# Second MLP product of an encoder layer: operands split in the units' order, weight sums issued four units ahead, and the last product's row tiles taken 0, 2, 1, 3

## The chip, the core and the metric
The kernel runs on one core of a Trainium2 chip. The metric is the device time of one execution in microseconds (us), as the median of several runs. Below, PE is the matrix engine, DVE the vector engine, ACT the scalar engine, POOL the general engine, and SP the engine whose queue issues most transfers.

## The reference
One layer of an encoder runs on two sequences of 512 rows and 1024 columns. After attention, retention and an output projection comes the MLP, and this change lies in its second product and in the final norm:

```python
h = rms_norm(x, norm2_g[l]) * (1.0 + sc2) + sh2
x = x + g2 * (jnp.square(jax.nn.relu(h @ w_mlp1[l])) @ w_mlp2[l])
return rms_norm(x, final_g)
```

The hidden width is 4096. All inputs are float32.

## The kernel before, in words
Every float32 product is made of three matmuls in a reduced format: an operand is split into a high part (a cast, on ACT) and a low part (source minus high part, on DVE), and high x high, high x low and low x high are added up in PSUM.

Both MLP products use a seven-product scheme for a 2 x 2 block split (Strassen's, in Winograd's form). The first product runs over 16 pairs of hidden tiles (`FirstPair`, PE line L933) and writes the seven combinations of the activations to DRAM (`spill`). The second product is the list `steps`: two groups g, in each the seven products in the order P1, P2, P6, P7, P5, P4, P3, and in each product NU = 4 units h. That makes 56 units, numbered n from 0. `multiply(n, t)` issues six matmuls of unit n for row tile t; a unit is 24 matmuls over four row tiles (L1291). The results stand in four PSUM tiles of two banks each: `x` and `y`, each for th = 0 (row tiles 0 and 1) and th = 1 (row tiles 2 and 3). P1, P6, P5 and P3 write `x`, the others `y`.

What a unit needs comes in three steps, each run ahead of it in the loop over n:
- `load_u(n + 4)` (L1248) loads the unit's activation `ur` from `spill`, and `load_w(n + 8)` (L1241) loads weight blocks. Only P1, P2 and P6 load: P1 block b11, P2 block b21, P6 blocks b12 and b22. All go through SP's queue.
- `prep(n + 2)` makes the operands. For a unit of P6 it first makes three sums of weight blocks on DVE (L1268 to L1270), for P7 one (L1272); P5, P4 and P3 reuse them. Then `split_pairs` splits activation (`uc_n_h`, `uc_n_l`) and weight (`wc_n_h`, `wc_n_l`): ACT line L838, DVE line L839.
- The split operands, the weight blocks and two of four sum tiles share a pool of 32 equal buffers (`r4`); four of them go to a unit's split.

A scheduler sets the order of the instructions on each engine here; program order is a preference, not a rule, except where `in_order` or `pin` fixes it. An engine takes its instructions strictly in that order.

After a product's last unit `gather` takes the bank: a copy on ACT (L1303) the first time, else an addition on DVE (L1305). In the last group the sums are multiplied by a gate row and added to the residual `x2r` (`gated`, L1332 and L1333), squared and summed along the row (`squares`: ACT L1338, POOL L1341), and scaled with the inverse root (`finish`: POOL L1345, then DVE L1352 or, for one half, ACT L1350) and stored (L1353, SP's queue).

The last product (P3 of group 1) is written out by row tiles: for each t in 0, 1, 2, 3 all four units, then `finish` of the rows that are ready, `gated`, `squares` and `finish(0, t)`. The pairs (i, t) name half and tile of the output rows. The order of this part is fixed by `pin`.

Of the kernel before, what the change touches and what calls it, by code (L numbers as in the profile page):

```python
# [13 lines left out]
ALU = mybir.AluOpType  # L14

P = 128
# [14 lines left out]
def trunk_kernel(ctx, tc, x0, x1, c0, c1, w_ada, b_ada, norm1_g, w_in, attn_sink, decay_f, decay_b,  # L31
                 w_out, norm2_g, w_mlp1, w_mlp2, final_g, y0, y1):
    nc = tc.nc
    xin = (x0[0], x1[0])
    yout = (y0[0], y1[0])
# [19 lines left out]
    def r4(name, dtype=F32R):  # L55
        return work.tile([P, 2, 512], dtype, tag="r4", name=name, bufs=N_R4)
# [7 lines left out]
    def junk(name):  # L64
        return work.tile([P, 1024], BF16, tag="f2", name=name, bufs=8)

    def small(shape, name, tag="small", bufs=24):
        return work.tile(shape, F32, tag=tag, name=name, bufs=bufs)

    def f(ap):  # L70
        return ap.bitcast(F32)
# [70 lines left out]
    neghalf = const.tile([P, 4], F32, name="neghalf")  # L142
# [9 lines left out]
    for r0, src in ((0, c0[0]), (8, c1[0]), (16, norm1_g[0]), (24, norm2_g[0]), (32, b_ada)):  # L152
        n = src.shape[0] // P
# [672 lines left out]
    P1, P2, P6, P7, P5, P4, P3 = range(7)  # L826
# [10 lines left out]
    def split_to(hi, lo, src):  # L837
        nc.scalar.copy(hi, src)  # L838
        nc.vector.tensor_sub(lo, src, f(hi))  # L839
# [21 lines left out]
    class FirstPair:  # L861
# [15 lines left out]
        def prep(self, p):  # L877
            r1, r2 = self.raw
            c = lambda t: t.rearrange("p (s k n) -> p s k n", s=2, n=P)
            w = lambda t: t.rearrange("p (k n) -> p k n", n=256)  # L880
            F1, F2 = slice(0, P), slice(P, 256)
            if p in (P1, P2):
                t = c(self.pair(f"a{p}", True))
                split_to(t[:, 0], t[:, 1], (r1 if p == P1 else r2)[:, :, F1])
                self.left[p] = t[:, 0], t[:, 1]
            elif p == P6:
                self.s1 = f2(f"ws1_{self.n}").rearrange("p (k n) -> p k n", n=P)
                nc.vector.tensor_tensor(self.s1, r1[:, :, F2], r2[:, :, F2], ALU.add)
                nc.vector.tensor_sub(r1[:, :, F2], r1[:, :, F1], r1[:, :, F2])
                nc.vector.tensor_sub(r1[:, :, F1], self.s1, r1[:, :, F1])  # L890
                h, l = w(self.pair("s2h", False)), w(self.pair("s2l", False))
                split_to(h, l, r1)
                self.left[P6] = h[:, :, F1], l[:, :, F1]
                self.left[P7] = h[:, :, F2], l[:, :, F2]
            elif p == P5:
                t = c(self.pair("s1", True))
                split_to(t[:, 0], t[:, 1], self.s1)
                self.left[P5] = t[:, 0], t[:, 1]
            elif p == P4:
                nc.vector.tensor_sub(r2[:, :, F1], r2[:, :, F1], r1[:, :, F1])  # L900
                h, l = w(self.pair("s4h", False)), w(self.pair("s4l", False))
                split_to(h, l, r2)
                self.left[P3] = h[:, :, F1], l[:, :, F1]
                self.left[P4] = h[:, :, F2], l[:, :, F2]
# [321 lines left out]
    steps = [(g, p, h) for g in range(NG) for p in ORDER for h in range(NU)]  # L1226
    blocks = {P1: [(0, 0)], P2: [(1, 0)], P6: [(0, 1), (1, 1)]}
    raw_w, raw_u, left, right, t1 = {}, {}, {}, {}, {}
    acc, fin = {}, {}
# [4 lines left out]
    def load_w(n):  # L1234
        if n >= len(steps):
            return
        g, p, h = steps[n]
        n0 = g * GP + 2 * h
        for k, j in blocks.get(p, ()):
            t = raw_w[g, k, j, h] = r4(f"w2_{g}_{h}_{k}{j}", F32)  # L1240
            nc.sync.dma_start(t, w_mlp2.rearrange("(n k p) c -> p n k c", k=2, p=P)[:, n0:n0 + 2, k, j * 512:(j + 1) * 512])  # L1241

    def load_u(n):
        if n >= len(steps):
            return
        g, p, h = steps[n]
        t = raw_u[n] = (r4 if n < NU else lx)(f"ur_{n}", F32)
        in_order(nc.sync.dma_start(t, spill[g][p, :, 2 * h:2 * h + 2, :]))  # L1248

    def split_pairs(name, src):  # L1250
        hi, lo = r4(f"{name}h"), r4(f"{name}l")
        split_to(hi, lo, src)
        return hi, lo

    def t1_tile(g, h):
        if h < 2:
            pool, tag, bufs = ((work, "raw", 3), (late, "ws2", 3))[h]
            return pool.tile([P, 2, 512], F32, tag=tag, name=f"t1_{g}_{h}", bufs=bufs)
        return r4(f"t1_{g}_{h}", F32)

    def prep(n):
        if n >= len(steps):
            return
        g, p, h = steps[n]
        b11, b12, b21, b22 = [raw_w.get((g, k, j, h)) for k in range(2) for j in range(2)]
        if p == P6:
            t = t1[g, h] = t1_tile(g, h)
            nc.vector.tensor_sub(t, b12, b11)  # L1268
            nc.vector.tensor_sub(b12, b22, b12)
            nc.vector.tensor_sub(b11, b22, t)  # L1270
        if p == P7:
            nc.vector.tensor_sub(b21, b21, b11)  # L1272
        src = {P1: b11, P2: b21, P6: b11, P7: b12, P5: t1.get((g, h)), P4: b21, P3: b22}[p]
        left[n] = split_pairs(f"uc_{n}_", raw_u.pop(n))
        right[n] = split_pairs(f"wc_{n}_", src)


    bank = {}
# [28 lines left out]
    def cols_of(j):  # L1307
        return slice(j * 512, (j + 1) * 512)
# [26 lines left out]
    def squares(q, t):  # L1335
        i, j = q
        ss = small([P, 1], f"ssf_{i}_{t}_{j}")
        nc.scalar.activation(junk(f"jkf_{i}_{t}_{j}")[:, :512], fin["x", i, t // 2, j][:, t % 2, :], AF.Square, accum_out=ss)  # L1338
        before = fin.get(("ms", i, t), EPS)
        ms = fin["ms", i, t] = small([P, 1], f"msf_{i}_{t}_{j}")  # L1340
        nc.gpsimd.tensor_scalar(ms, ss, 1.0 / D, before, ALU.mult, ALU.add)  # L1341

    def finish(i, t, gained=()):
        r = small([P, 1], f"rf_{i}_{t}")
        nc.gpsimd.tensor_tensor(r, fin["ms", i, t], neghalf[:, 0:1], ALU.pow)  # L1345
        r0 = i * 256 + (t % 2) * P
        for j in range(2):
            x = fin["x", i, t // 2, j][:, t % 2, :]
            if j in gained:
                nc.scalar.activation(x, x, AF.Copy, scale=r)  # L1350
            else:
                nc.vector.scalar_tensor_tensor(x, x, r, fin["f", j], ALU.mult, ALU.mult)  # L1352
            nc.sync.dma_start(yout[t // 2][r0:r0 + P, cols_of(j)], x)  # L1353


    ahead = {P1: lambda: (load_w(0), load_u(0), load_w(1), load_u(1)),
# [21 lines left out]
    for n, (g, p, h) in enumerate(steps[:-NU]):  # L1378
        final = g == NG - 1
        load_u(n + 4)  # L1380
        load_w(n + 8)
        prep(n + 2)
        if n + NU + 1 == len(steps):
            prep(n + 3)
            prep(n + 4)
        if final and h == 0:
            if p == P1:
                final_loads()
            elif p == P7:
                final_rows(0)  # L1390
            elif p == P5:
                final_rows(1)
        for t in range(4):
            src = multiply(n, t)
            th = t // 2
            if h < NU - 1 or t % 2 == 0:
                continue
            q = where[p]
            if not final or p in (P1, P6, P7):
                gather(p, th, src)  # L1400
            elif p == P2:
                gather(p, th, src)
            elif p == P5:
                gather(p, th, src)
                gated(q, th, acc[q, th])
            else:
                gated(q, th, src)
        if final and p in (P7, P5, P4) and h == NU - 1:
            if p == P7:
                for th in range(NB):  # L1410
                    gated((0, 0), th, acc[(0, 0), th])
                for t in range(4):
                    squares((0, 0), t)
            elif p == P5:
                for q in ((1, 0), (0, 1)):
                    for th in range(NB):
                        gated(q, th, acc[q, th])
                for t in range(4):
                    squares((1, 1), t)
            else:  # L1420
                for t in range(4):
                    squares((1, 0), t)
    start = len(nc.cur_bb.bb.instructions)
    for t in range(4):
        for n in range(len(steps) - NU, len(steps)):
            src = multiply(n, t)
        if t == 0:
            finish(1, 0)
            finish(1, 1)
        elif t == 1:  # L1430
            finish(1, 2)
            finish(1, 3)
        elif t == 3:
            x = fin["x", 0, 1, 0][:, 1, :]
            nc.vector.tensor_tensor(x, x, fin["f", 0], ALU.mult)
        gated((0, 1), t // 2, src[:, t % 2:t % 2 + 1, :], slice(t % 2, t % 2 + 1))
        squares((0, 1), t)
        finish(0, t, (0,) if t == 3 else ())
    pin(start)
    lates.close()  # L1440
    front.close()
# [27 lines left out]
```

## Time and profile before

| | |
|---|---|
| median of 3 runs | 1148.64 us (1148.45 to 1151.57) |
| the profiled execution | 1147.91 us, span 1145.2 us |
| PE busy | 1111.3 us, 97% of the span |
| DVE, ACT, POOL busy | 889.1, 506.8, 46.8 us |
| mean granted clock of PE | 0.991 |
| second product, first and last matmul | 819.2 and 1136.8 us |

The time outside the span is 2.7 us. Times below are microseconds from the start of the span. In a row of the timeline stand start, duration, engine, line, operation, output<-inputs and, in brackets, the idle time before it with what ended it. Matmuls overlap, so the step from one start to the next is what a matmul costs, not its duration. In names, buffer and unit numbers are left out (`wc_l<-w,wc_h`: the low part of a weight).

### The profile page before, as it was taken

To read this page: it belongs to the slowest core of one execution; us is meant where nothing else is said; L and a number is where in the kernel's file an instruction comes from. 1 tells how busy PE (TensorE), PEld (TensorE's weight loads), DVE (VectorE), ACT (ScalarE), POOL (GpSimd) and SP (SyncE) were. 2 spreads that over 40 slices of the span, in tenths; PEclk is the share of its full clock that TensorE was granted. 3 is DMA by queue.
4 is the path that set the end of the run, shared out by engine and by line. 5 is a ranking of instruction groups with operands and counts; after the bars stand their busy time and mean duration, and the time that the engine had idled before them with its cause. 6 is when DMAs were issued, how large, how long until landed. Compare 5 with 4: busy or idle time off the path is not lost.

```text
span 1145.2 us, 14502 instructions
## 1 busy us (share of the span) xinstructions
PE 1111.3 (97%) x5205; PEld 909.7 (79%) x5205; DVE 889.1 (78%) x1484; ACT 506.8 (44%) x860; POOL 46.8 (4%) x82
## 2 busy tenths in 40 slices
PE   7899999999999999999999999999989999999996
PEld 5688887778888778887888888888868888888875
DVE  6768888989878797689998779776768645688675
ACT  7737765444662334346333333333344542444341
POOL 2200001000000000100000000000000000000011
PEclk8999999999999999999999999999989999999998
DMA  9946767675555589941654445442883455524603
GB/s 309 377 179 206 236 207 278 190 230 177 164 174 186 163 307 346 320 147 49 220 200 157 169 168 187 157 165 102 307 315 104 138 201 196 199 91 167 194 14 142
DMA packets 124623, 224.36 MB, mean 196 GB/s; under 512 B 8500, under 2 KB 59780, under 8 KB 124552
## 3 DMA queue, kind: packets, MB, share of 16 engines
q1 hardware_dynamic: 122792, 217.09, 56.2%
q0 software_dynamic: 1632, 6.32, 1.5%
q8 instruction: 40, 0.66, 0.2%
q14 instruction: 31, 0.25, 0.1%
q10 hardware_dynamic: 128, 0.04, 0.0%
HBM read 152.36 MB, written 71.06 MB: 195 GB/s over the span
## 4 chain that ended last, share of the span: by engine, by line
PE 81%; DVE 8%; DMA 6%; ACT 2%; issue 2%; POOL 1%; SPq 0%; ACTq 0%; POOLq 0%; DVEq 0%
PE x L1291 13%; PE px_None L933 12%; PE y L1291 12%; PE py_None L933 9%; PE po L130 2%; PE po L131 2%; PE po L129 2%; PE po L421 2%; PE ppt L414 2%; PE psc L388 1%; DMA raw_ada<-in_w_ada_dram 1%; PE pj_rv L129 1%; PE pj_rv L130 1%; PE pj_rv L131 1%; PE pj_rg L129 1%
## 5 line engine op out<-in xcount | busy, mean ns | idle before, releaser
L839 DVE TENSOR_TENSOR uc_l<-ur,uc_h 128x1024 fp32r<-128x1024 f32 x56 | 68.3, 1220 | 49.0 <-ACT uc_h L838 31.9
L1291 PE MATMUL x<-wc_h,uc_h 128*128 128x512 f32 x256 | 100.4, 393 | 3.7 <-DVE acc L1332 3.7
L1291 PE MATMUL x<-wc_l,uc_h 128*128 128x512 f32 x256 | 100.2, 391 | 0.0
L1291 PE MATMUL x<-wc_h,uc_l 128*128 128x512 f32 x256 | 100.1, 391 | 0.0
L838 ACT CAST uc_h<-ur 128x1024 fp32r<-128x1024 f32 x56 | 58.8, 1050 | 77.5 <-PE x L1291 22.7
L1291 PE MATMUL y<-wc_l,uc_h 128*128 128x512 f32 x192 | 76.1, 396 | 4.3 <-DVE wc_l L839 4.3
L1291 PE MATMUL y<-wc_h,uc_l 128*128 128x512 f32 x192 | 75.8, 395 | 0.0
L1291 PE MATMUL y<-wc_h,uc_h 128*128 128x512 f32 x192 | 75.6, 394 | 0.0
L838 ACT CAST wc_h<-w 128x1024 fp32r<-128x1024 f32 x48 | 50.4, 1051 | 48.6 <-PE x L1291 19.4
L839 DVE TENSOR_TENSOR wc_l<-w,wc_h 128x1024 fp32r<-128x1024 f32 x48 | 58.5, 1218 | 6.5 <-ACT wc_h L838 4.5
L1291 PEld LDWEIGHTS x<-wc_h,uc_h 128*128 128x128 f32 x256 | 48.4, 189 | 14.6 <-DVE acc L1332 4.5
L1291 PEld LDWEIGHTS x<-wc_l,uc_h 128*128 128x128 f32 x256 | 48.5, 189 | 10.1
L1291 PEld LDWEIGHTS x<-wc_h,uc_l 128*128 128x128 f32 x256 | 48.4, 189 | 10.1
L129 PE MATMUL po<-wh_wo,ms 128*128 128x512 f32 x128 | 50.5, 397 | 1.3 <-ACT ms L757 1.3
L130 PE MATMUL po<-wl_wo,ms 128*128 128x512 f32 x128 | 49.8, 391 | 1.0 <-DVE wl_wo L103 1.0
L131 PE MATMUL po<-wh_wo,ms 128*128 128x512 f32 x128 | 49.6, 390 | 0.0
L1291 PEld LDWEIGHTS y<-wc_l,uc_h 128*128 128x128 f32 x192 | 36.7, 191 | 12.5 <-DVE wc_l L839 4.7
L244 DVE SCALAR_TENSOR_TENSOR adacc_c<-raw_ada_c,cact,adacc_c 128x512 f32<-128x512 f32 x56 | 39.8, 744 | 7.5 <-DMA raw_ada_c<-in_w_ada_dram 6.5
L838 ACT CAST wc_s4h<-raw_w 128x1024 fp32r<-128x1024 f32 x16 | 16.8, 1052 | 62.2 <-PE px_None L933 41.3
L398 ACT ACTIVATE st<-st,negm 128x256 f32<-128x256 f32 (+1 forms) x64 | 35.2, 556 | 18.4 <-DVE negm L393 18.4
L1291 PEld LDWEIGHTS y<-wc_h,uc_h 128*128 128x128 f32 x192 | 36.7, 191 | 7.8
L1291 PEld LDWEIGHTS y<-wc_h,uc_l 128*128 128x128 f32 x192 | 36.7, 191 | 7.6
(391 smaller groups left out, 3065.3 us busy)
## 6 DMA issues: line engine op xcount, KB each, us to landing
ur<-spill SPq DMA_DIRECT2D x56, 512.0 KB, 4.6
raw_w<-in_w_mlp_dram SPq DMA_DIRECT2D x32, 512.0 KB, 3.7
spill<-s SPq DMA_DIRECT2D x64, 256.0 KB, 3.2
w<-in_w_mlp_dram SPq DMA_DIRECT2D x32, 512.0 KB, 5.9
spill<-u SPq DMA_DIRECT2D x48, 256.0 KB, 2.3
raw_ada_g<-in_w_ada_dram SPq DMA_DIRECT2D x16, 512.0 KB, 4.5
raw_ada_c<-in_w_ada_dram SPq DMA_DIRECT2D x16, 512.0 KB, 3.7
raw_ada<-in_w_ada_dram SPq DMA_DIRECT2D x12, 512.0 KB, 11.0
```

Of the source, the lines that this page charges most:

```text
L129: nc.tensor.matmul(ps, lhs[0], rhs[0], start=start, stop=False)
L130: nc.tensor.matmul(ps, lhs[0], rhs[1], start=False, stop=False)
L131: nc.tensor.matmul(ps, lhs[1], rhs[0], start=False, stop=stop)
L244: nc.vector.scalar_tensor_tensor(acc[b], src, cb, acc[b], ALU.mult, ALU.add)
L388: nc.tensor.matmul(psc[:, :w], qs[hh][:, isl], k_[:, s, j0 * P:j1 * P], start=(s == 0), stop=(s == 1))
L398: nc.scalar.activation(st[hh][:, :w], st[hh][:, :w], AF.Exp, bias=negm[:, hh:hh + 1], scale=0.125, accum_out=den[:, hh:hh + 1])
L414: nc.tensor.transpose(pt[:, hh * P:(hh + 1) * P], st[hh][:, jj * P:(jj + 1) * P], ident)
L421: nc.tensor.matmul(po, va[:, j0 + jj, g].rearrange("p s e -> p (s e)"), pts[jj][:, s, :], start=(jj == 0 and s == 0), stop=(jj == nj - 1 a ...
L838: nc.scalar.copy(hi, src)
L839: nc.vector.tensor_sub(lo, src, f(hi))
L933: self.last = nc.tensor.matmul(bank[:, cs], x[:, k, :], y, start=first and k == 0 and i == 0, stop=last and k == 3 and i == 2, skip_group_ ...
L1291: nc.tensor.matmul(out, left[n][x][:, i, ts_], right[n][y][:, i, :], start=first and i == 0 and k == 0, stop=end and i == 1 and k == 2, sk ...
```

## The change
1. Splits are kept in the units' order. `prep` runs under `issue_after` for the last split: on ACT and on DVE nothing of unit n + 1's split may stand ahead of unit n's.
2. The weight sums leave `prep`. A new function `combine`, called for unit n + 4 ahead of `prep(n + 2)`, issues them behind the split of unit n + 1; the split of unit n + 2 then stands behind them on DVE.
3. P6's blocks are loaded seven units ahead instead of eight; P1's and P2's stay at eight.
4. The last product takes its row tiles in the order 0, 2, 1, 3. The inverse roots are computed in `factor`, right behind the squares, and `finish` only scales and stores. Two scalings follow each of the tiles 0, 2 and 1 (`ends`): rows (1, 3) and rows (0, t) are scaled one tile later than before. The last tile's half that ACT scales is stored from ACT's queue instead of SP's.

```diff
-        split_to(hi, lo, src)
+        last_split[:] = [nc.scalar.copy(hi, src), nc.vector.tensor_sub(lo, src, f(hi))]
...
     def prep(n):
...
+        with ExitStack() as behind:
+            for i in readied:
+                behind.enter_context(tc.issue_after(i))
+            split_unit_of(n)
+
+    def combine(n):
...
+        with ExitStack() as behind:
+            for i in readied:
+                behind.enter_context(tc.issue_after(i))
+            if p == P6:
+                t = t1[g, h] = t1_tile(g, h)
+                nc.vector.tensor_sub(t, b12, b11)
+                nc.vector.tensor_sub(b12, b22, b12)
+                x = nc.vector.tensor_sub(b11, b22, t)
+            else:
+                x = nc.vector.tensor_sub(b21, b21, b11)
+        readied[:] = [readied[0], x.ins]
...
+        readied[:] = [x.ins for x in last_split]
...
+    def factor(i, t):
+        r = fin["r", i, t] = small([P, 1], f"rf_{i}_{t}")
+        nc.gpsimd.tensor_tensor(r, fin["ms", i, t], neghalf[:, 0:1], ALU.pow)
+
     def finish(i, t, gained=()):
-        r = small([P, 1], f"rf_{i}_{t}")
-        nc.gpsimd.tensor_tensor(r, fin["ms", i, t], neghalf[:, 0:1], ALU.pow)
+        r = fin["r", i, t]
...
-            nc.sync.dma_start(yout[t // 2][r0:r0 + P, cols_of(j)], x)
+            (nc.scalar if j in gained else nc.sync).dma_start(yout[t // 2][r0:r0 + P, cols_of(j)], x)
...
-        load_w(n + 8)
+        for lead, kinds in ((8, (P1, P2)), (7, (P6,))):
+            if n + lead < len(steps) and steps[n + lead][1] in kinds:
+                load_w(n + lead)
+        combine(n + 4)
         prep(n + 2)
...
+                for t in range(4):
+                    factor(1, t)
...
-    for t in range(4):
+    ends = {0: ((1, 0), (1, 1)), 2: ((1, 2), (0, 0)), 1: ((1, 3), (0, 2)), 3: ((0, 1), (0, 3))}
+    for t in (0, 2, 1, 3):
...
+        if t != 3:
+            for e in ends[t]:
+                finish(*e)
+        else:
+            finish(*ends[t][0])
             x = fin["x", 0, 1, 0][:, 1, :]
             nc.vector.tensor_tensor(x, x, fin["f", 0], ALU.mult)
...
-        finish(0, t, (0,) if t == 3 else ())
+        factor(0, t)
+    finish(0, 3, (0,))
```

Three places show what it moves. First DVE, at the second product's units 3 to 5. `uc_n` and `wc_n` are unit n's operands, `t1_0_h` and `w2_0_h_kj` the sums and weight blocks of group 0, unit h. Before:

```order
L839 TENSOR_TENSOR uc_3_l_7806<-ur_3_7690,uc_3_h_7805 128x1024
L839 TENSOR_TENSOR wc_3_l_7810<-w2_0_3_00_7688,wc_3_h_7809 128x1024
L1268 TENSOR_TENSOR t1_0_1_8027<-w2_0_1_01_7801,w2_0_1_00_7622 128x1024
L1269 TENSOR_TENSOR w2_0_1_01_7801<-w2_0_1_11_7803,w2_0_1_01_7801 128x1024
L1270 TENSOR_TENSOR w2_0_1_00_7622<-w2_0_1_11_7803,t1_0_1_8027 128x1024
L839 TENSOR_TENSOR uc_4_l_7844<-ur_4_7759,uc_4_h_7843 128x1024
L839 TENSOR_TENSOR wc_4_l_7848<-w2_0_0_10_7706,wc_4_h_7847 128x1024
L1268 TENSOR_TENSOR t1_0_0_7989<-w2_0_0_01_7761,w2_0_0_00_7618 128x1024
```

In the changed kernel:

```order
L1254 TENSOR_TENSOR uc_3_l_7802<-ur_3_7690,uc_3_h_7801 128x1024
L1254 TENSOR_TENSOR wc_3_l_7806<-w2_0_3_00_7688,wc_3_h_7805 128x1024
L1254 TENSOR_TENSOR uc_4_l_7840<-ur_4_7759,uc_4_h_7839 128x1024
L1254 TENSOR_TENSOR wc_4_l_7844<-w2_0_0_10_7706,wc_4_h_7843 128x1024
L1254 TENSOR_TENSOR uc_5_l_7878<-ur_5_7795,uc_5_h_7877 128x1024
L1254 TENSOR_TENSOR wc_5_l_7882<-w2_0_1_10_7708,wc_5_h_7881 128x1024
L1284 TENSOR_TENSOR t1_0_0_7919<-w2_0_0_01_7797,w2_0_0_00_7618 128x1024
L1285 TENSOR_TENSOR w2_0_0_01_7797<-w2_0_0_11_7799,w2_0_0_01_7797 128x1024
L1286 TENSOR_TENSOR w2_0_0_00_7618<-w2_0_0_11_7799,t1_0_0_7919 128x1024
L1254 TENSOR_TENSOR uc_6_l_7924<-ur_6_7833,uc_6_h_7923 128x1024
L1254 TENSOR_TENSOR wc_6_l_7928<-w2_0_2_10_7724,wc_6_h_7927 128x1024
```

The splits of units 4 and 5 moved ahead of the first sums, and the sums of a unit now stand between the splits of two units.

Second ACT, at the end of P1 in group 0, where the two PSUM tiles `x_0_0_0` and `x_0_0_1` are copied out. Before:

```order
L838 CAST wc_4_h_7847<-w2_0_0_10_7706 128x1024
L1303 COPY acc_00_0_7901<-x_0_0_0_7773 128x1024
L838 CAST uc_5_h_7881<-ur_5_7799 128x1024
L1303 COPY acc_00_1_7915<-x_0_0_1_7786 128x1024
L838 CAST wc_5_h_7885<-w2_0_1_10_7708 128x1024
```

In the changed kernel:

```order
L1254 CAST wc_4_h_7843<-w2_0_0_10_7706 128x1024
L1326 COPY acc_00_0_7897<-x_0_0_0_7769 128x1024
L1326 COPY acc_00_1_7911<-x_0_0_1_7782 128x1024
L1254 CAST uc_5_h_7877<-ur_5_7795 128x1024
L1254 CAST wc_5_h_7881<-w2_0_1_10_7708 128x1024
```

Unit 5's first cast moved behind the second copy.

Third DVE in the last product; `x_1_0_0` is the PSUM tile of row tiles 0 and 1, `x_1_0_1` that of 2 and 3, and `rf_i_t` the inverse root of output rows (i, t). Before, from the scaling of rows (1, 1):

```order
L1352 SCALAR_TENSOR_TENSOR x2r_1_0_1_9441<-x2r_1_0_1_9441,rf_1_1_9813,fgain_1_8815 128x512
L1332 TENSOR_TENSOR acc_01_0_8775<-x_1_0_0_8817,fgate_0_1_8811 128x512
L1333 TENSOR_TENSOR x2r_0_0_1_9268<-x2r_0_0_1_9268,acc_01_0_8775 128x512
L1352 SCALAR_TENSOR_TENSOR x2r_0_0_0_9266<-x2r_0_0_0_9266,rf_0_0_9826,fgain_0_8809 128x512
L1352 SCALAR_TENSOR_TENSOR x2r_0_0_1_9268<-x2r_0_0_1_9268,rf_0_0_9826,fgain_1_8815 128x512
L1352 SCALAR_TENSOR_TENSOR x2r_1_1_0_9443<-x2r_1_1_0_9443,rf_1_2_9856,fgain_0_8809 128x512
L1352 SCALAR_TENSOR_TENSOR x2r_1_1_1_9445<-x2r_1_1_1_9445,rf_1_2_9856,fgain_1_8815 128x512
L1352 SCALAR_TENSOR_TENSOR x2r_1_1_0_9443<-x2r_1_1_0_9443,rf_1_3_9862,fgain_0_8809 128x512
L1352 SCALAR_TENSOR_TENSOR x2r_1_1_1_9445<-x2r_1_1_1_9445,rf_1_3_9862,fgain_1_8815 128x512
L1332 TENSOR_TENSOR acc_01_0_8775<-x_1_0_0_8817,fgate_0_1_8811 128x512
```

In the changed kernel:

```order
L1378 SCALAR_TENSOR_TENSOR x2r_1_0_1_9441<-x2r_1_0_1_9441,rf_1_1_9785,fgain_1_8811 128x512
L1355 TENSOR_TENSOR acc_01_0_8775<-x_1_0_0_8813,fgate_0_1_8807 128x512
L1356 TENSOR_TENSOR x2r_0_0_1_9269<-x2r_0_0_1_9269,acc_01_0_8775 128x512
L1378 SCALAR_TENSOR_TENSOR x2r_1_1_0_9443<-x2r_1_1_0_9443,rf_1_2_9787,fgain_0_8805 128x512
L1378 SCALAR_TENSOR_TENSOR x2r_1_1_1_9445<-x2r_1_1_1_9445,rf_1_2_9787,fgain_1_8811 128x512
L1378 SCALAR_TENSOR_TENSOR x2r_0_0_0_9267<-x2r_0_0_0_9267,rf_0_0_9830,fgain_0_8805 128x512
L1378 SCALAR_TENSOR_TENSOR x2r_0_0_1_9269<-x2r_0_0_1_9269,rf_0_0_9830,fgain_1_8811 128x512
L1355 TENSOR_TENSOR acc_01_1_8789<-x_1_0_1_8826,fgate_1_1_8809 128x512
```

The second gating reads the other PSUM tile, and the scaling of rows (0, 0) stands behind that of (1, 2).

More of the change, by code (lines that the diff above doesn't have):

```diff
@@ L1248, in load_u @@
         in_order(nc.sync.dma_start(t, spill[g][p, :, 2 * h:2 * h + 2, :]))
+    readied, last_split = [], []
     def split_pairs(name, src):
         hi, lo = r4(f"{name}h"), r4(f"{name}l")
-        split_to(hi, lo, src)
+        last_split[:] = [nc.scalar.copy(hi, src), nc.vector.tensor_sub(lo, src, f(hi))]
         return hi, lo
@@ L1263, in prep, with split_unit_of @@
             return
+        with ExitStack() as behind:
[3 more added lines that the diff above has]
+    def combine(n):
+        if n >= len(steps):
+            return
+        g, p, h = steps[n]
+        if p not in (P6, P7):
+            return
+        b11, b12, b21, b22 = [raw_w.get((g, k, j, h)) for k in range(2) for j in range(2)]
+        with ExitStack() as behind:
[9 more added lines that the diff above has]
+        readied[:] = [readied[0], x.ins]
+    def split_unit_of(n):
         g, p, h = steps[n]
         b11, b12, b21, b22 = [raw_w.get((g, k, j, h)) for k in range(2) for j in range(2)]
[L1266 to L1272, printed above, removed]
         src = {P1: b11, P2: b21, P6: b11, P7: b12, P5: t1.get((g, h)), P4: b21, P3: b22}[p]
@@ L1422, in trunk_kernel @@
                     squares((1, 0), t)
+                for t in range(4):
+                    factor(1, t)
     start = len(nc.cur_bb.bb.instructions)
-    for t in range(4):
+    ends = {0: ((1, 0), (1, 1)), 2: ((1, 2), (0, 0)), 1: ((1, 3), (0, 2)), 3: ((0, 1), (0, 3))}
+    for t in (0, 2, 1, 3):
         for n in range(len(steps) - NU, len(steps)):
             src = multiply(n, t)
[L1427 to L1433, printed above, removed]
+        if t != 3:
[3 more added lines that the diff above has]
+            finish(*ends[t][0])
             x = fin["x", 0, 1, 0][:, 1, :]
```

## The prediction
> **What bounds the kernel now.** I read the page first, then the waits of TensorE alone.
>
> ```profile
> span 1145.2 us, 14502 instructions
> PE 1111.3 (97%) x5205; PEld 909.7 (79%) x5205; DVE 889.1 (78%) x1484; ACT 506.8 (44%) x860; POOL 46.8 (4%) x82
> ```
> ```profile
> PE y L1291 <- DVE wc_l L839: 4.3, 1, 4.3
> PE x L1291 <- DVE acc L1332: 3.7, 2, 2.9
> ```
> PE is busy in 97% of the span, so only its own idle time, its clock, and what follows its last matmul can be won. The two waits at the head of its list (total, times, longest) are both in the second MLP product: one of 4.3 us for a split weight, two for the gating of a bank. The windows show the clock there and, for comparison, around a 1.72 us gap of the first product; columns are us, busy time of PE, PEld, DVE, ACT and POOL, then granted clock, DMA share and GB/s.
>
> ```profile
> 516.00:521.00 5.00, 3.28 (x29) 3.08 (x28) 5.00 (x8) 5.00 (x10) 0.00 (x0) 1.00 0.00 0
> ...
> 827.00:840.00 13.00, 13.00 (x59) 10.78 (x58) 1.77 (x3) 3.55 (x4) 0.00 (x0) 1.00 1.05 395
> 840.00:852.00 12.00, 7.69 (x22) 5.77 (x22) 11.81 (x11) 6.25 (x7) 0.00 (x0) 0.72 0.94 339
> ...
> 1115.00:1122.00 7.00, 4.11 (x12) 3.24 (x12) 5.09 (x9) 0.73 (x2) 2.06 (x5) 0.76 0.40 150
> ```
> Behind each long wait the clock fell (0.72, 0.76); behind the 1.72 us gap it stayed at 1.00:
>
> ```profile
> 519.45 0.39 PE L933 MATMUL px<-hcl,wc_a 128*128 128x256 f32 x1 [1.72 <-DVE hcl L839]
> ```
> So a long wait is paid twice.
>
> **Part 1: units in order, sums ahead.** The timeline of PE at the second product's unit 4 (first of P2; a unit is 24 matmuls):
>
> ```profile
> 840.97 0.39 PE L1291 MATMUL y<-wc_h,uc_h 128*128 128x512 f32 x1
> 845.67 0.79 PE L1291 MATMUL y<-wc_l,uc_h 128*128 128x512 f32 x1 [4.31 <-DVE wc_l L839]
> ...
> 851.74 0.39 PE L1291 MATMUL y<-wc_h,uc_h 128*128 128x512 f32 x1
> ...
> 1114.69 0.39 PE L1291 MATMUL x<-wc_h,uc_l 128*128 128x512 f32 x1
> 1117.96 0.80 PE L1291 MATMUL x<-wc_h,uc_h 128*128 128x512 f32 x1 [2.89 <-DVE acc L1332]
> ...
> 1121.44 0.39 PE L1291 MATMUL x<-wc_h,uc_l 128*128 128x512 f32 x1
> ...
> 1130.28 0.39 PE L1291 MATMUL x<-wc_h,uc_l 128*128 128x512 f32 x1
> 1131.45 0.50 PE L1291 MATMUL x<-wc_h,uc_h 128*128 128x512 f32 x1 [0.78 <-DVE acc L1332]
> ...
> 1136.84 0.39 PE L1291 MATMUL x<-wc_h,uc_l 128*128 128x512 f32 x1
> ```
> From 1121.44 to 1130.28 are 39 steps, so a matmul costs 0.2267 us and a unit 5.44. The matmul at 851.74 is the fifteenth after 840.97; without wait and slow clock it starts at 840.97 + 15 x 0.2267 = 844.37. The price of the wait is 7.37 us: 4.47 of standing, 2.90 of half-rate matmuls. What DVE and ACT did:
>
> ```profile
> 827.12 1.22 DVE L839 TENSOR_TENSOR wc_l<-w,wc_h 128x1024 fp32r<-128x1024 f32 x1
> 839.57 1.22 DVE L1268 TENSOR_TENSOR t<-w,w 128x1024 f32<-128x1024 f32 x1 [11.23 <-DMA w<-in_w_mlp_dram]
> 840.98 1.23 DVE L1269 TENSOR_TENSOR w<-w,w 128x1024 f32<-128x1024 f32 x1 [0.19 <-DMA w<-in_w_mlp_dram]
> 842.12 1.22 DVE L1270 TENSOR_TENSOR w<-w,t 128x1024 f32<-128x1024 f32 x1
> 843.26 1.22 DVE L839 TENSOR_TENSOR uc_l<-ur,uc_h 128x1024 fp32r<-128x1024 f32 x1
> 844.39 1.22 DVE L839 TENSOR_TENSOR wc_l<-w,wc_h 128x1024 fp32r<-128x1024 f32 x1
> ```
> ```profile
> 834.27 1.05 ACT L838 CAST uc_h<-ur 128x1024 fp32r<-128x1024 f32 x1 [8.84 <-DMA ur<-spill]
> 835.23 1.04 ACT L838 CAST wc_h<-w 128x1024 fp32r<-128x1024 f32 x1
> ...
> 841.16 1.01 ACT L1303 COPY acc<-x 128x1024 f32<-128x1024 f32 x1 [0.76 <-PE x L1291]
> 842.07 1.05 ACT L838 CAST wc_h<-w 128x1024 fp32r<-128x1024 f32 x1
> ```
> DVE stood 11.23 us at a sum for P6 whose weight block was in flight; unit 4's subtractions, whose high halves ACT had ready at 836.27, stood behind it. In the new order both come first: they run from 835.4 to 837.7, 3.5 us before PE wants the second (841.20). The wait goes, -7.37.
>
> What is late next. On ACT both bank copies now stand ahead of unit 5's casts, and the second cannot start before 841.16 (PE's last matmul of P1). So unit 5's casts start at 842.07 and 843.02, and DVE, idle since 837.7, starts its subtraction at 843.15. From there it has no slack: to the end of unit 8's split are 17 operations (8 splits, 9 sums), 1.137 us apart as from 842.12 to 844.39; the second sum of each three rewrites a block that the first has just read and I step it like a dependent pair, 1.26, from these two rows:
>
> ```profile
> 1109.67 1.22 DVE L1332 TENSOR_TENSOR acc<-y,fgate 128x1024 f32<-128x1024 f32 x1 [0.24 <-PE y L1291]
> 1110.93 1.23 DVE L1333 TENSOR_TENSOR x2r<-x2r,acc 128x1024 f32<-128x1024 f32 x1
> 1114.57 2.74 DVE L1352 SCALAR_TENSOR_TENSOR x2r<-x2r,rf,fgain 128x512 f32<-128x512 f32 x4 [2.42 <-POOL rf L1345]
> 1117.22 0.68 DVE L1332 TENSOR_TENSOR acc<-x,fgate 128x512 f32<-128x512 f32 x1
> ...
> 1120.51 4.07 DVE L1352 SCALAR_TENSOR_TENSOR x2r<-x2r,rf,fgain 128x512 f32<-128x512 f32 x6 [1.87 <-POOL rf L1345]
> ...
> 1137.27 0.69 DVE L1332 TENSOR_TENSOR acc<-x,fgate 128x512 f32<-128x512 f32 x1 [1.25 <-PE x L1291]
> ```
> Unit 8 is split at 843.15 + 13 x 1.137 + 3 x 1.26 + 1.22 = 862.93; PE wants it at 841.20 + 96 x 0.2267 = 862.96: just in time. Unit 9 takes six more (three sums, a bank addition, two splits), 869.75 against 868.40: PE waits 1.35. Unit 10 takes four, 4.55 of the 5.44 us, and DVE draws ahead. Waiting instructions between the operations make it a little more: I take +1.5. Its ends are 0 (ACT's casts slip ahead of the copy) and +4.5 (a wait like the 2.89 with its slow clock).
>
> The loads. Unit 5's operand is now issued ahead of the first pair of P6 blocks, one pair later for that pair:
>
> ```profile
> 826.12 0.32 SPq L1248 DMA_DIRECT2D ur<-spill  x1
> 827.51 1.70 SPq L1241 DMA_DIRECT2D w<-in_w_mlp_dram  x2
> 830.53 0.34 SPq L1248 DMA_DIRECT2D ur<-spill  x1
> ```
> The second pair in the old order had landed by 840.98, behind two operands; the new first sum wants the first pair at 845.4. DMA is full there (share 1.05), but these are the same bytes, so nothing: the cover is those 4.4 us. Group 1's sums move four units later too. At worst 12 sums, 8 splits and 4 bank operations fall into four units: 24 x 1.137 = 27.3 us in 21.8, 5.5 too many. DVE's lead has to cover that. In the waits of the second product, the casts wait mostly for PE:
>
> ```profile
> ACT uc_h L838 <- PE x L1291: 22.7, 6, 4.4
> ACT uc_h L838 <- PE y L1291: 22.3, 6, 5.5
> ```
> That is a wait for PE to free a buffer: operands lie as far ahead as there is room, and with 32 such buffers, 18 of them held by weights and sums and four to a unit, that is over two units beside the one in use (10.9 us). I cost it at 0; without that lead it is +5.5.
>
> **Part 2: row tiles 0, 2, 1, 3.** Tiles 0 and 1 share one PSUM tile, 2 and 3 the other. Before, tile 1 waited (1117.96) until DVE, behind four scalings (1114.57), had gated tile 0; now tile 2 needs no such wait and tile 1 starts 5.44 us later. From 1114.69 the remaining 72 matmuls take 16.32 us: the last starts at 1131.01 instead of 1136.84, -5.83. It consists of 3.04 + 0.94 of standing, 1.67 of slow clock (eight matmuls from 1117.96 to 1121.44 in 3.48 us) and a rest of 0.18.
>
> The Trainium skill ("TensorE: Matmul & The Clock Gate", What's actually happening) lets the clock fall only after an idle window of about 3.4 us. By it the 2.89 us gap would have kept the full rate, part 2 would bring the 1.67 us of slow matmuls from 1117.96 to 1121.44 less, 4.16, and the sum below would be 9.9 instead of 11.6. Here the measurement decides: the 0.76 stands behind that gap.
>
> After the last matmul DVE gates tile 3. In the new order it is less free. Gating to scaling is 1120.51 - 1117.22 = 3.29 us. Scalings of (0, 0) end at 1121.9, so tile 2 is gated then; its own scalings run from 1125.2 to 1126.55, so tile 1 is gated at 1126.55 (PE done: 1126.0), its scalings run from 1129.84 to 1131.2 and the final gain to 1131.9, where PE would allow 1131.01 + 0.43 = 1131.44. I take +0.3 (ends 0, and +0.8 if the chain runs half a microsecond later still). The inverse roots are computed earlier on POOL, whose queue is free then: 0. The last two stores:
>
> ```profile
> 1141.30 0.81 SPq L1353 DMA_DIRECT2D out_dram<-x2r  x2
> ```
> One of them now leaves from ACT's queue beside the other: half of 0.81 at best, and no row prices such an issue there, so +0.4 to -0.4; nearest is the row itself, -0.2.
>
> **Sum:** -7.37 + 1.5 - 5.83 + 0.3 - 0.2 = -11.6. The profiled execution took 1147.91: 1136.3. The median of the runs is 0.73 above it, 1148.64: 1137.0.
>
> **Rivals.**
> A. The short waits at units 8 and 9 lower the clock. For it: DVE arrives with hundredths to spare, so several gaps in 10 us are possible. Against: 0.78 and 1.72 left it at 1.00. Cost 1.67 (as behind 1117.96) to 2.90 (as behind 845.67): 1138.7 to 1139.9. The Trainium skill has it on the same page, "A second HAM failure mode: psum-queue depth-cycling": many short idles between groups make the clock swing. No gap of this trace shows that.
> B. Tile 2 waits like tile 1 did, because its bank's last reader is also late on DVE. Against: that was the P5 sum, long past. Part 2 then brings nothing: 1142.8.
> C. Unit 4 stays late, since DVE waits for something else in its new queue. Against: everything it needs was there at 836.27. Part 1 brings nothing: 1142.9.
> D. Slower. DVE's order now puts all splits behind sums that wait for DMA; if a P6 block lands late, unit 6 and everything behind it stand. Each us after 845.4 costs one, and 2.9 more for the clock: 1148.64 + 0.3% = 1152.1 needs a landing at 857.6, 16.6 us after the second pair's in the old order. For it: the full DMA. Against: 4.4 us of cover with unchanged bytes.
>
> **How the numbers follow.** Forecast 0.82 (1135 to 1139), A 0.08, B 0.03, C 0.03, D 0.02, and 0.02 for anything between the old time and B. About 0.3% (3.4 us) is what a measurement of this kernel can tell from no change. B and C still lie 5.7 below: faster 0.96, same 0.02, slower 0.02. The range 1134.5 to 1140.5 reaches from no new wait and the better ends of the tail (1148.64 - 7.37 - 5.83 - 0.4 = 1135.0), with half a microsecond for the spread of the runs on either side, over A.
>
> **What would show it.** PE's list loses both waits and has instead one of 1 to 2 us for wc_l in P6 (x). The clock is 1.00 from 840 to 872 and up to the last matmul, which starts near 1136.84 - 11.7 = 1125.1; the span is near 1133.6. DVE's subtraction of unit 5 starts near 843. I am wrong in part 1 if units 5 to 9 wait several times or over 2.5 us, in part 2 if any matmul of the last product waits for gating, in the tail if it is longer than the old 1145.2 - 1136.84 = 8.4 by over 0.5.

## The result, and the profile after

The changed kernel takes 1138.50 us (median of 5 runs, 1137.52 to 1139.88), the kernel before 1148.64 (1144.04 to 1151.57). The ratio is 0.9911, 95% interval 0.9883 to 0.9939: faster, by 10.1 us on the medians where 11.6 were forecast. The profiled execution took 1137.64 us. The head of its page, and the list of PE's waits from the second product on:

```profile
span 1135.6 us, 14507 instructions
PE 1105.9 (97%) x5205; PEld 905.9 (80%) x5205; DVE 888.8 (78%) x1484; ACT 506.8 (45%) x860; POOL 53.2 (5%) x82
```
```profile
PE x L1314 <- DVE wc_l L1254: 0.8, 1, 0.8
```

The 4.3 us wait of P2 and the two waits for gating are gone. One new wait for a split weight is left. The windows (us; PE, PEld, DVE, ACT, POOL; granted clock; DMA share; GB/s) have the clock at 1.00 throughout:

```profile
840.00:852.00 12.00, 12.00 (x55) 9.93 (x54) 7.35 (x7) 9.73 (x10) 0.00 (x0) 1.00 1.01 381
852.00:872.00 20.00, 19.15 (x84) 15.31 (x83) 19.93 (x18) 7.06 (x7) 0.00 (x0) 1.00 0.31 92
1104.00:1113.00 9.00, 9.00 (x42) 7.44 (x40) 6.32 (x8) 2.67 (x8) 4.41 (x8) 1.00 0.16 61
1113.00:1128.00 15.00, 13.76 (x61) 11.07 (x59) 11.43 (x18) 2.17 (x6) 2.96 (x6) 1.00 0.52 195
```

In the second row DVE is busy for 19.93 of 20 us: it has become the bound there. Spans of two executions are hard to compare at this scale, because the second product doesn't begin at the same time. I therefore split each span at two matmuls, its first and its last: "product" is from one start to the other, "end" from the last start to the end of the span.

| kernel | median, us | span | first matmul | product | end |
|---|---|---|---|---|---|
| before | 1148.64 | 1145.2 | 819.2 | 317.63 | 8.36 |
| changed | 1138.50 | 1135.6 | 820.6 | 305.76 | 9.23 |
| `units_only` | 1142.57 | 1140.6 | 820.6 | 311.61 | 8.41 |
| `rows_only` | 1141.68 | 1139.6 | 820.1 | 310.31 | 9.22 |
| `rows_in_sequence` | 1139.42 | 1137.7 | 820.9 | 308.02 | 8.76 |
| `casts_first` | 1135.78 | 1133.0 | 819.3 | 304.42 | 9.26 |
| `gate_first` | 1137.85 | 1137.2 | 823.0 | 305.78 | 8.45 |
| `sp_store` | 1138.41 | 1136.9 | 822.0 | 305.78 | 9.17 |
| `both_moves` | 1135.58 | 1134.3 | 821.5 | 304.41 | 8.39 |
| `scalings_beside` | 1136.09 | 1134.8 | 821.8 | 304.41 | 8.60 |

The instructions ahead of the first matmul are the same in all ten kernels, yet it stands between 819.2 and 823.0. Between kernels that are alike there, the product and the end repeat to 0.06 us (305.76, 305.78, 305.78), with one exception: the wait at unit 4, which cost 1.5 us less in `rows_only` than in the kernel before. The two stretches, not the medians, carry the experiments.

From before to after the span loses 9.6 us: 11.87 in the product, while the end grows by 0.87 and the part ahead of both by 1.4.

Two readings of the trace lead to the experiments. First, what remains in the product: 1343 steps of 0.2267 are 304.46, so 1.30 of the 305.76 are lost. PE's timeline has both places, units 8 and 9:

```profile
864.43 0.50 PE L1314 MATMUL x<-wc_l,uc_h 128*128 128x512 f32 x1
864.77 0.39 PE L1314 MATMUL x<-wc_h,uc_l 128*128 128x512 f32 x1
...
871.24 0.50 PE L1314 MATMUL x<-wc_l,uc_h 128*128 128x512 f32 x1 [0.85 <-DVE wc_l L1254]
```

Unit 8's matmul is 0.2 late without being listed as a wait; unit 9 brings the other 1.1. On DVE, and on ACT ahead of it, this begins 20 us earlier:

```profile
837.50 1.22 DVE L1254 TENSOR_TENSOR wc_l<-w,wc_h 128x1024 fp32r<-128x1024 f32 x1
844.61 1.23 DVE L1254 TENSOR_TENSOR uc_l<-ur,uc_h 128x1024 fp32r<-128x1024 f32 x1 [5.90 <-ACT uc_h L1254]
...
846.89 1.22 DVE L1284 TENSOR_TENSOR t<-w,w 128x1024 f32<-128x1024 f32 x1
848.14 1.23 DVE L1285 TENSOR_TENSOR w<-w,w 128x1024 f32<-128x1024 f32 x1
```
```profile
840.07 1.02 ACT L1326 COPY acc<-x 128x1024 f32<-128x1024 f32 x1 [2.79 <-PE x L1314]
842.62 1.01 ACT L1326 COPY acc<-x 128x1024 f32<-128x1024 f32 x1 [1.53 <-PE x L1314]
843.53 1.05 ACT L1254 CAST uc_h<-ur 128x1024 fp32r<-128x1024 f32 x1
844.48 1.05 ACT L1254 CAST wc_h<-w 128x1024 fp32r<-128x1024 f32 x1
```

DVE stands for 5.90 us, since unit 5's cast stands behind the second bank copy, which can't start before PE ends P1.

Second, the end. The chain that ended last, by line from 1100 on and then its pieces in order of time, no longer runs through PE after 1105.02:

```profile
by line: DVE x2r L1378 19.7%; PE y L1314 14.5%; DVE x2r L1356 11.2%; ACT jkf L1361 10.6%; DVE acc L1355 10.2%; issue 6.8%; POOL rf L1368 6.1%; POOL msf L1364 5.2%; DVE x2r L1465 1.7%; POOLq L1496 1.7%; ACTq L1361 0.4%; POOLq L1364 0.0%
1099.79 5.23 PE y L1314 x23
1105.02 0.02 issue
1105.04 1.24 DVE acc L1355
```

From there on the last product is one row of gating, squares, root and scaling over DVE, ACT and POOL, and PE runs beside it. On DVE's timeline:

```profile
1112.60 0.68 DVE L1355 TENSOR_TENSOR acc<-x,fgate 128x512 f32<-128x512 f32 x1
1113.31 0.69 DVE L1356 TENSOR_TENSOR x2r<-x2r,acc 128x512 f32<-128x512 f32 x1
1113.92 1.41 DVE L1378 SCALAR_TENSOR_TENSOR x2r<-x2r,rf,fgain 128x512 f32<-128x512 f32 x2
1116.13 1.42 DVE L1378 SCALAR_TENSOR_TENSOR x2r<-x2r,rf,fgain 128x512 f32<-128x512 f32 x2 [0.80 <-POOL rf L1368]
1117.46 0.68 DVE L1355 TENSOR_TENSOR acc<-x,fgate 128x512 f32<-128x512 f32 x1
...
1122.32 0.69 DVE L1355 TENSOR_TENSOR acc<-x,fgate 128x512 f32<-128x512 f32 x1
...
1127.54 0.68 DVE L1355 TENSOR_TENSOR acc<-x,fgate 128x512 f32<-128x512 f32 x1
```
```profile
1126.37 0.39 PE L1314 MATMUL x<-wc_h,uc_l 128*128 128x512 f32 x1
```

The last gating starts 1.17 after the last matmul's start; before it was 0.43 (1137.27 against 1136.84). That is 0.74 of the 0.87. The rest lies behind the last scaling: from its start to the end of the span are 4.79 us (1135.6 - 1130.81), before 4.65 (1145.2 - 1140.55).

### The profile page after: what moved, and what is told of

It is laid out like the page before. It is cut to its first block, busy times and chain, and to the rows that moved or that the text cites. A ratio compares the mean times of both kernels' runs of the same rounds, so it can differ in the third digit from the quotient of the medians.

```text
span 1135.6 us, 14507 instructions
## 1 busy us (share of the span) xinstructions
PE 1105.9 (97%) x5205; PEld 905.9 (80%) x5205; DVE 888.8 (78%) x1484; ACT 506.8 (45%) x860; POOL 53.2 (5%) x82
## 4 chain that ended last, share of the span: by engine, by line
PE 80%; DVE 10%; DMA 4%; issue 2%; ACT 2%; POOL 1%; ACTq 0%; POOLq 0%; SPq 0%; DVEq 0%
PE px_None L933 13%; PE x L1314 13%; PE py_None L933 10%; PE y L1314 10%; PE po L130 2%; PE po L131 2%; PE po L129 2%; PE po L421 2%; PE ppt L414 2%; PE psc L388 1%; DMA raw_ada<-in_w_ada_dram 1%; PE pj_rv L129 1%; PE pj_rv L130 1%; PE pj_rv L131 1%; PE pj_rg L129 1%
## 5 line engine op out<-in xcount | busy, mean ns | idle before, releaser
L1314 PEld LDWEIGHTS x<-wc_l,uc_h 128*128 128x128 f32 x256 | 48.0, 188 | 11.6 <-DVE wc_l L1254 1.6
```

The costliest lines, as they stand in the source:

```text
L1314: nc.tensor.matmul(out, left[n][x][:, i, ts_], right[n][y][:, i, :], start=first and i == 0 and k == 0, stop=end and i == 1 and k == 2, sk ...
```

## The experiments

**One part at a time.** `units_only` has the changed kernel's order of splits, sums and loads, with the last product and the last store as before; `rows_only` has the reverse. The first as a diff against the changed kernel:

```diff
-    for t in (0, 2, 1, 3):
+    for t in range(4):
...
-            for e in ends[t]:
-                finish(*e)
...
+        finish(0, t, (0,) if t == 3 else ())
```

> Part 1 alone (splits in the units' order, sums ahead, P6's loads seven ahead); the last product is as before. Theory (the parts add): from the first to the last matmul of the second product, 317.64 us before and 305.76 after, part 1 took 7.37 off and put 1.30 on, so here 311.6; no wait at unit 4, the short ones at units 8 and 9, and both waits for gating (2.9 and 0.8) with the slow clock behind the first. From the last matmul to the end of the span 8.4, as before. In all 6.1 less than before, near 1142.5. Rival (the parts work through one another: with DVE's new order the gating is reached earlier or later): that stretch is off by over 0.5 us.

Measured: 1142.57 us, ratio 0.996 (0.9939 to 0.9982); product 311.61, end 8.41. PE's waits from the second product on:

```profile
PE x L1314 <- DVE acc L1355: 3.7, 2, 2.9
PE x L1314 <- DVE wc_l L1254: 0.8, 1, 0.8
```

As the theory had it, to the tenth. For `rows_only`, against the kernel before:

```diff
-    for t in range(4):
+    ends = {0: ((1, 0), (1, 1)), 2: ((1, 2), (0, 0)), 1: ((1, 3), (0, 2)), 3: ((0, 1), (0, 3))}
+    for t in (0, 2, 1, 3):
```

> Part 2 alone (row tiles 0, 2, 1, 3, scalings one tile later, last store from ACT); splits and sums are as before. Theory (the parts add): first to last matmul 317.64 - 5.83 = 311.8; the 4.3 us wait at unit 4 with its clock of 0.72 stays, no matmul waits for gating. From the last matmul to the end 9.2, as after and not 8.4 as before, since what made it longer lies in this part. In all 5.0 less than before, near 1143.6. Rival (the longer end comes from elsewhere, from the execution or from part 1): 8.4 there, 1142.8.

Measured: 1141.68 us, ratio 0.9943 (0.9924 to 0.9963); product 310.31, end 9.22. The longer end belongs to this part. The product is 1.5 shorter than expected, and PE's timeline at unit 4 says why:

```profile
846.20 0.50 PE L1291 MATMUL y<-wc_l,uc_h 128*128 128x512 f32 x1 [3.98 <-DVE wc_l L839]
...
846.89 0.63 PE L1291 MATMUL y<-wc_h,uc_h 128*128 128x512 f32 x1
...
849.88 0.46 PE L1291 MATMUL y<-wc_l,uc_h 128*128 128x512 f32 x1
850.18 0.39 PE L1291 MATMUL y<-wc_h,uc_l 128*128 128x512 f32 x1
```

The wait was 0.33 shorter than before's 4.31, but the slow matmuls ended after 4.0 us instead of 6.1 (845.67 to 851.74). The granted clock was at 0.50 for 3.4 us here and for 6.8 us before (the last section has the rows). So the price of unit 4's wait was 310.31 - 304.46 = 5.85 here and 7.37 before, though the work around it is the same: the parts add, except for this price.

**Was it the tile order or DVE's queue?** `rows_in_sequence` takes the tiles 0, 1, 2, 3 again, and gates each tile ahead of all scalings that it needn't wait for:

```diff
-    ends = {0: ((1, 0), (1, 1)), 2: ((1, 2), (0, 0)), 1: ((1, 3), (0, 2)), 3: ((0, 1), (0, 3))}
-    for t in (0, 2, 1, 3):
+    ends = {1: ((1, 0), (1, 1)), 2: ((1, 2), (1, 3)), 3: ((0, 0), (0, 1))}
+    for t in range(4):
...
+    finish(0, 2)
     finish(0, 3, (0,))
```

> The changed kernel with row tiles 0, 1, 2, 3, but with each tile's gating on DVE ahead of all scalings that it needn't wait for. Theory 1 (the long wait was DVE's queue, four scalings ahead of the gating; the tile order only hides the gating itself): tiles 1 and 3 wait about 0.9 us each, the clock stays at 1.00, first to last matmul 305.76 + 1.9 = 307.7, and the end is 8.4, not 9.2, since DVE is free when the last tile is done: near 1139.5. Theory 2 (the tile order itself removes both waits): the wait of 2.9 us and its slow clock come back, 305.76 + 5.65 = 311.4, near 1143.3.

Measured: 1139.42 us, ratio 0.9917 (0.9895 to 0.9938); product 308.02, end 8.76. Both waits are there, both short, and the clock stays (timeline of PE, then the window around the first):

```profile
1111.55 0.50 PE L1314 MATMUL x<-wc_h,uc_h 128*128 128x512 f32 x1 [0.78 <-DVE acc L1355]
...
1123.55 0.50 PE L1314 MATMUL x<-wc_h,uc_h 128*128 128x512 f32 x1 [0.78 <-DVE acc L1355]
```
```profile
1106.00:1113.00 7.00, 6.22 (x28) 4.81 (x27) 3.98 (x6) 2.56 (x8) 4.11 (x8) 1.00 0.00 0
```

Theory 1 holds. Of part 2's 5.8 us, 3.6 (311.61 - 308.02) come from gating ahead of four scalings, without any change of tile order; the order 0, 2, 1, 3 brings the remaining 2.3 (308.02 - 305.76), the price of two gatings that can't be hidden while a tile writes the PSUM tile that is being read. The end is longer than the 8.4 expected; the last section says why.

**The wait at unit 9.** `casts_first` makes the second bank copy of P1 follow unit 5's casts on ACT:

```diff
-            nc.scalar.copy(acc[q, th], src)
+            with ExitStack() as behind:
+                if q == (0, 0) and th == 1:
+                    behind.enter_context(tc.issue_after(readied[0]))
+                nc.scalar.copy(acc[q, th], src)
```

> The changed kernel with one move on ACT: the casts of unit 5 stand ahead of the second bank copy of P1, not behind it. Theory (unit 5's split starts late because of that copy, and this sets the waits at units 8 and 9): DVE starts unit 5's subtraction 2.5 us earlier against PE, and the 1.30 us of waits at units 8 and 9 are gone; first to last matmul 304.5 instead of 305.8, near 1137.2. Rival (DVE then waits for P6's blocks instead): DVE stands before a sum until its block has landed, and 305.8 stays.

Measured: 1135.78 us, ratio 0.9884 (0.986 to 0.9909); product 304.42, and no wait of PE in the whole second product. ACT and DVE:

```profile
838.79 1.02 ACT L1329 COPY acc<-x 128x1024 f32<-128x1024 f32 x1 [2.89 <-PE x L1314]
839.70 1.05 ACT L1254 CAST uc_h<-ur 128x1024 fp32r<-128x1024 f32 x1
840.65 1.05 ACT L1254 CAST wc_h<-w 128x1024 fp32r<-128x1024 f32 x1
841.60 1.01 ACT L1329 COPY acc<-x 128x1024 f32<-128x1024 f32 x1
```
```profile
840.79 1.23 DVE L1254 TENSOR_TENSOR uc_l<-ur,uc_h 128x1024 fp32r<-128x1024 f32 x1 [3.44 <-ACT uc_h L1254]
841.93 1.22 DVE L1254 TENSOR_TENSOR wc_l<-w,wc_h 128x1024 fp32r<-128x1024 f32 x1
843.06 1.22 DVE L1284 TENSOR_TENSOR t<-w,w 128x1024 f32<-128x1024 f32 x1
```

The start is 2.5 earlier against PE (5.90 of idle time has become 3.44), and the first sum follows without a wait, so P6's blocks had landed even for this earlier time. The cause of the 1.30 us is shown: one copy in ACT's queue.

**The longer end.** `gate_first` moves two scalings and the gain on DVE:

```diff
-    ends = {0: ((1, 0), (1, 1)), 2: ((1, 2), (0, 0)), 1: ((1, 3), (0, 2)), 3: ((0, 1), (0, 3))}
+    ends = {0: ((1, 0), (1, 1)), 2: ((1, 2), (1, 3)), 1: ((0, 0),), 3: ((0, 2), (0, 1))}
...
             nc.vector.tensor_tensor(x, x, fin["f", 0], ALU.mult)
+            finish(*ends[t][1])
```

> The changed kernel with two scalings moved on DVE in the last product: rows (0, 0) are scaled behind the gating of tile 2 and rows (0, 2) behind that of tile 1, and the last half's gain multiplication stands ahead of the scalings of (0, 1). Theory (the longer end is DVE's lateness: from the last matmul to the last gating 1.17 us in the changed kernel, 0.43 before): the last gating starts 0.43 us after the last matmul's start, and the end shrinks from 9.23 to 8.5; first to last matmul 305.8 as in the changed kernel. Rival 1 (the end is longer because the store leaves from ACT): 9.2 stays. Rival 2 (the chain gating, squares, root, scaling of tile 1 is too long for 5.44 us however it is ordered): the last gating still comes about 1 us after the last matmul.

Measured: 1137.85 us, ratio 0.9896 (0.9866 to 0.9926); product 305.78, end 8.45. The last gating (DVE) stands 0.43 behind the last matmul's start at 1128.75:

```profile
1129.18 0.69 DVE L1355 TENSOR_TENSOR acc<-x,fgate 128x512 f32<-128x512 f32 x1
```

`sp_store` has the last store back on SP's queue:

```diff
-            (nc.scalar if j in gained else nc.sync).dma_start(yout[t // 2][r0:r0 + P, cols_of(j)], x)
+            nc.sync.dma_start(yout[t // 2][r0:r0 + P, cols_of(j)], x)
```

> The changed kernel with the last store back on SP's queue. From the start of the last scaling to the end of the span are 4.65 us before and 4.70 with part 1 alone (SP), 4.79 to 4.82 in the three kernels that store from ACT. Theory (the ACT store gains nothing): 4.65 to 4.70 here, the end 9.1 instead of 9.23. Rival (the prediction's -0.2 holds): 4.9 to 5.0, the end 9.4.

Measured: 1138.41 us, ratio 0.9907 (0.9873 to 0.9941); product 305.78, end 9.17. From the last scaling (1132.21) to the end of the span are 4.69 us. With the ACT store it was 4.73 to 4.82 in the changed kernel, `rows_only`, `rows_in_sequence`, `casts_first` and `gate_first`, with SP 4.63 to 4.70 in the kernel before and the other three that store from SP. The spans are given to 0.1 us, so the difference is at the limit of what can be read; a gain of 0.2 it is not.

**All moves, and one move taken back.** `both_moves` joins the three edits above.

> The changed kernel with the three moves together: unit 5's casts ahead of the second bank copy, gating ahead of the scalings that it needn't wait for, last store from SP. Theory (they add): first to last matmul 304.4, end 8.4, so 2.2 us less than the changed kernel, near 1136.3 for a median of 1138.5. Rival (one gives back what another brings): stretch and end differ by over 0.4 us from these.

Measured: 1135.58 us (1134.94 to 1136.13), ratio 0.988 (0.9856 to 0.9903); product 304.41, end 8.39. They add: 2.19 us less than the changed kernel in the two stretches. Its runs all lie below those of the changed kernel, though those were taken at another time and the two intervals against the kernel before overlap. Of the kernels here its product and end together are the shortest, 312.80; its median can't be told from those of `casts_first` (1135.78) and `scalings_beside` (1136.09).

`scalings_beside` differs from it in one point: rows (0, 1) are scaled behind the last gating.

```diff
-            finish(*ends[t][1])
...
+    finish(0, 1)
     finish(0, 3, (0,))
```

> As the kernel with the three moves, but DVE scales rows (0, 1) behind the last gating, in the 1.87 us in which it otherwise waits for the last inverse root. Theory (POOL's small operations run slower while DVE scales: the sum of squares took 0.52 and 0.54 us for tiles 0 and 2, where DVE scaled, 0.26 for tiles 1 and 3, where DVE stood): it takes 0.5 us here, and the end is 0.25 us longer than in the kernel with the three moves, 8.65 for 8.4. Rival (the 0.52 is chance, or set by POOL's own queue): 0.26, and the end is the same to 0.1.

Measured: 1136.09 us, ratio 0.9886 (0.9858 to 0.9913); product 304.41, end 8.60, 0.21 longer. POOL's last sum of squares in `both_moves`, and in this kernel with DVE's scalings ahead of it:

```profile
1128.70 0.27 POOL L1367 TENSOR_SCALAR msf<-ssf,msf 128x1 f32<-128x1 f32 x1 [3.76 <-ACT jkf L1364]
```
```profile
1127.96 1.41 DVE L1381 SCALAR_TENSOR_TENSOR x2r<-x2r,rf,fgain 128x512 f32<-128x512 f32 x2
...
1128.99 0.52 POOL L1367 TENSOR_SCALAR msf<-ssf,msf 128x1 f32<-128x1 f32 x1 [3.77 <-ACT jkf L1364]
```

The work is the same, the time twice as long, and the difference reaches the end of the span.

## Why the prediction was right, and where a term was off

- *The wait at unit 4, -7.37:* right. It is gone with its slow clock, and `units_only` shows part 1 on its own: 317.63 - 311.61 = 6.02, against 7.37 - 1.30 = 6.07. That the size fits so well is in part luck: 7.37 is the price in one execution of the kernel before, and in `rows_only` the same wait cost 5.85.
- *The new wait at units 8 and 9, +1.5 (1.35 by hand):* right, 1.30, though the list has it as one wait of 0.8 where the prediction named 1 to 2 us as the sign. Unit 5's subtraction was forecast for 843.15 and came at 844.61 with the second product 1.4 later; unit 8 was just in time, short of 0.2. The step of 1.26 for the dependent sum is 848.14 - 846.89 = 1.25. The reason given, the second copy, is the one that `casts_first` removes.
- *Loads 0, group 1's sums 0:* right; in `casts_first` the blocks were even there 2.5 us earlier, and no wait of PE lies in group 1.
- *Part 2, -5.83:* right in size (317.63 - 7.37 + 1.30 - 5.83 = 305.73, measured 305.76). Its account of the tile order was incomplete: the long wait needed only another order on DVE.
- *The end, +0.3 - 0.2:* this step failed; it is +0.87, more than the 0.5 that the prediction gave as the sign of being wrong in the tail. The gating of tile 3 came 0.74 late where the working gave 0.46 and I took 0.3. The working had 3.29 us from gating to scaling for each tile. In the changed kernel tiles 0 and 2 took 3.53 (1116.13 - 1112.60, 1120.99 - 1117.46), because POOL's sum took 0.52 and 0.54 beside DVE's scalings instead of 0.26. These two add 0.5 to the working, and its other steps were 0.2 shorter in all. The scalings moved behind the gating thus lengthened the chain that they wait for. The store from ACT, put at -0.2, brought nothing (`sp_store`).
- *Rivals:* A is false, the clock is 1.00 behind the new waits, and behind two of 0.78 in `rows_in_sequence`. For B and C, no tile waits and unit 4 isn't late. D's late block didn't come.
- *The rest of the 1.5 us* between 1137.0 and 1138.5: the two stretches give -11.0, which from 1148.64 is 1137.6. The other 0.9 lies within the scatter of the front of the program. What sets that scatter stays open.

## What to carry to other kernels

When a long wait of PE is removed, look for the engine that has no slack behind it and at the instruction that starts its run: here a bank copy, needed by nobody for 20 us, stood ahead of a cast for which everything waited. Ahead of changing the order of tiles, see whether the reader that frees the PSUM tile merely stands behind work that could wait; that gave 3.6 of 5.8 us. And when the last matmuls are no longer waited for, follow the chain of the trailing work: its period must be below the tile's, and it must not start late.

## What the runs showed of the hardware that was not expected

POOL and DVE get in each other's way. POOL's 128x1 sum of squares takes 0.26 to 0.27 us while DVE stands, and beside a pair of DVE's scalings it ends shortly behind them: in `scalings_beside` at 1129.51, where the scalings end at 1129.37. In the changed kernel it is the same for tiles 0 and 2:

```profile
1114.95 0.52 POOL L1364 TENSOR_SCALAR msf<-ssf,msf 128x1 f32<-128x1 f32 x1 [3.19 <-ACT jkf L1361]
...
1119.79 0.54 POOL L1364 TENSOR_SCALAR msf<-ssf,msf 128x1 f32<-128x1 f32 x1 [3.69 <-ACT jkf L1361]
1124.67 0.26 POOL L1364 TENSOR_SCALAR msf<-ssf,msf 128x1 f32<-128x1 f32 x1 [3.72 <-ACT jkf L1361]
```

The first ends at 1115.47, DVE's scalings at 1115.33; for the third, DVE stands. In `rows_in_sequence`, where a pair of scalings followed the last gating, it took 0.52 too, which explains 0.25 of the 0.4 by which that end exceeded its expectation; the rest lies behind the last scaling, 4.79 us with the store from ACT as in the changed kernel. The Trainium skill ("SBUF — State Buffer", SBUF: two separate sides) says that VectorE and GpSimd (DVE and POOL here) share a port pair as an exclusive lock, so that the later one blocks until the other's instruction has ended, also where VectorE reads two inputs from SBUF. The rows of the pairs agree: the sum ends 0.13 to 0.14 us behind DVE's second scaling. And beside DVE's L1355 with `y`, where one of the two inputs lies in PSUM, the sum took 0.26 (changed kernel, at 1105.80 beside 1105.04 to 1106.26).

Longer runs on DVE don't fit so simply. Beside four scalings (`rows_in_sequence`; DVE, then POOL) the sum took 1.10 us:

```profile
1112.14 2.74 DVE L1378 SCALAR_TENSOR_TENSOR x2r<-x2r,rf,fgain 128x512 f32<-128x512 f32 x4
```
```profile
1113.17 1.10 POOL L1364 TENSOR_SCALAR msf<-ssf,msf 128x1 f32<-128x1 f32 x1 [1.38 <-ACT jkf L1361]
```

It starts during the second scaling, as in a pair, but ends at 1114.27, when two scalings more have begun and the run still goes on to 1114.88. Which instruction of a longer run lets the sum in stays open.

The clock's price came in steps. Behind the gap of 4.31 us (before) the granted clock stood at 0.50 for 6.8 us, behind those of 3.98 (`rows_only`), 2.90 (`units_only`) and 2.89 us (before, at the gating) for 3.4 us each. The first and the last window of 1 us of such a stretch, before and in `rows_only`; all windows between them are at 0.50:

```profile
844.00:845.00 1.00, 0.00 (x0) 0.00 (x0) 1.00 (x2) 1.00 (x2) 0.00 (x0) 0.91 1.00 385
...
851.00:852.00 1.00, 1.00 (x5) 0.82 (x4) 1.00 (x2) 0.00 (x0) 0.00 (x0) 0.68 0.71 221
```
```profile
846.00:847.00 1.00, 0.81 (x3) 0.67 (x4) 1.00 (x2) 0.23 (x1) 0.00 (x0) 0.80 1.06 389
...
850.00:851.00 1.00, 1.00 (x6) 0.82 (x5) 1.00 (x2) 0.00 (x0) 0.00 (x0) 0.99 1.01 332
```

A window with the clock at 0.91 has 0.09 / 0.50 = 0.18 us at half rate. So these are 0.18 + 6 + 0.64 = 6.8 us and 0.40 + 3 + 0.02 = 3.4 us. The longer one began 0.85 us before PE went on at 845.67, the shorter one 0.4 us after PE went on at 846.20. So a wait that was a third of a microsecond shorter cost 1.5 us less, while waits of 2.90 and 3.98 had stretches of one length. One gap of 0.85 and two of 0.78 left the clock at 1.00. What decides between one stretch and two, and what between 0.85 and 2.89 is free in this stage, was not tried.
